# A hybrid decoder step on one Trainium2 core: split weights kept in DRAM, SSD products on two column tiles, another order for the last piece, and finer sample parts

## The chip, the cores and the metric

The kernel runs on one core of one Trainium2 chip. The metric is the device time of one launch in microseconds (us), as the median of several runs. The engines go by the names of the profile: PE (TensorE's matmuls) and PEld (its weight loads), DVE (VectorE), ACT (ScalarE), POOL (GpSimd) and SP (SyncE, whose queue issues every DMA of this kernel).

## The reference

One layer of a decoder with two parallel groups of heads, over a prompt of 2048 tokens and over 8 sample sequences of 4 tokens each, which start from given states. Everything is float32.

```python
D_MODEL, SEQ, DEC_BATCH, DEC_SEQ, CHUNK = 1024, 2048, 8, 4, 64
SSD_HEADS, SSD_HEAD_DIM, SSD_GROUPS, SSD_STATE = 16, 64, 2, 128
GDN_HEADS, GDN_HEAD_DIM, CONV_K = 8, 128, 4

def _layer(x, c, conv_s, h_ssm, conv_g, S_gdn, ...):
    shift, scale, gate = split(silu(c) @ w_ada + b_ada, 3)
    h = rmsnorm(x, norm_w) * (1 + scale) + shift
    z_s, xbc_raw, dt_raw, z_g, qkv_raw, a_raw, b_raw = split(h @ w_in, IN_SIZES)
    xbc, new_conv_s = causal_conv(xbc_raw, conv_s, ssd_conv_w, ssd_conv_b)      # conv of 4 taps, then silu
    y, new_h = ssd(xs, softplus(dt_raw + ssd_dt_bias), -exp(ssd_a_log), Bm, Cm, h_ssm)
    y = grouped_rmsnorm((y + xh * ssd_d) * silu(z_s), ssd_norm_w)
    qkv, new_conv_g = causal_conv(qkv_raw, conv_g, gdn_conv_w, None)
    q, k = l2norm(q) * 128 ** -0.5, l2norm(k)
    o, new_S = gated_delta(q, k, v, -exp(gdn_a_log) * softplus(a_raw + gdn_dt_bias), sigmoid(b_raw), S_gdn)
    o = rmsnorm(o, gdn_norm_w) * silu(z_g)
    return x + gate * (concat([y, o]) @ w_out), new_conv_s, new_h, new_conv_g, new_S

# ssd, per chunk:          y = ((C B^T) * L) (x dt) + exp(acum) C h;    h = h d + B^T (decay x dt)
# gated_delta, per chunk:  (I + M) [u, w] = rhs (a triangular solve);   v_new = u - w S
#                          o = q_dec S + (q k^T * decay) v_new;         S = S d + k_dec^T v_new
```

A final RMSNorm follows. The outputs are the tokens of prompt and samples and the new states of both.

## The kernel before, in words

**Arithmetic.** The two large projections run as three matmuls in the type float32r: each operand is split into a high part (a cast) and a low part (the rest after the cast is subtracted), and high x high, low x high and high x low are summed. The other products are plain float32 matmuls, each of which the profile shows as two passes (two matmul records, each with its weight load).

**In-projection.** The prompt is cut into 4 pieces of 512 tokens; the 32 sample tokens go with the last piece (so its conv tiles have 544 columns, done as twice 272). The columns of w_in are 52 blocks of 128. A block's weights are used in halves (4 of the 8 blocks along the model dimension, 256 KB), 104 halves a piece and 416 in all. `want(i0)` is called before half i0 is used and fetches up to `NH` = 4 halves ahead: a DMA into `xin` (3 buffers), a cast to `whi` on ACT (L488) and a subtraction to `wlo` on POOL (L489), 4 buffers each. Every piece loads and splits the same 104 halves again. A `conv_tile` uses two halves and ends in the causal conv on ACT and DVE (L525 to L538); in the last piece both halves are used for the first 272 columns, and then again for the rest. A `z_pair` uses four halves for two gate blocks (L608).

**The order of work.** TensorE works in exactly the order in which the code is emitted. `at(tau, f)` puts each step at a place of a common scale, 106 steps to a piece, and all steps are then emitted in the order of tau. For the other engines and for SP's queue a planner sets the order when the program is built, and `hold` only keeps a step behind what was emitted before it. The conv tiles and z pairs are the fills: 24 matmuls that need only weights, between which the steps of the chains below lie.

**Gated DeltaNet, `gdn_pair`**, four pairs of heads a piece, each a long chain: six conv tiles at so, transposes (L675) and k products (L737, L738), the triangular solve, in which U goes through DRAM into another layout (`ud`, `ul`), is solved by 31 small steps on DVE (`lane`, L779 to L786), goes back through DRAM (`dd`), and is put together by five small products (b2_0 to b2_4, L811 to L853), and then four chunks of three `hop`s each, which pass the state on: p1 (L866), p2 (L878) and p3 (L885), with DVE or ACT between them. The arguments `e` and `dch` of a pair set where the hops start and how many steps of tau lie between two.

**SSD, `ssd_group`**, two groups of eight heads a piece, four chunks of 128 tokens each: `load` and `decay` (POOL, ACT) make the decay matrices L, `first` transposes and scales, `second` multiplies (L1019, L1022), and `third` updates the state (L1032). L1022 is eight products, one a head: a 128 x 128 weight, 64 moving columns.

**The end.** After the fills of piece 3 come the last SSD chunks, the last hops and `ada_gate` (L195). Then the out-projection starts: `units`, each of which transposes a quarter of a token tile (`turn_q`) and runs 24 matmuls as two `mm_half`s (L1162); during the first 8 units w_out is loaded, scaled and split (`load_wo`, L1133, L1134, L237, L238). From the ninth unit on, after each unit, one step of `sample()` is taken: a generator that works through the 8 sample sequences (`gdn_sample` and `ssd_sample`), stopping at each `yield`. Its state updates multiply a masked operand `RS` (one buffer, made by four ACT instructions, L1284) into PSUM (L1416) and add it to the state.

## Time and profile before

| | |
|---|---|
| median of 3 runs | 2392.36 us (2386.32 to 2394.52) |
| the profiled execution | 2388.52 us, of which the span from the first to the last instruction is 2386.8 us |
| mean granted TensorE clock | 0.975 of full speed |
| busy: PE, DVE, POOL, ACT | 2235.7, 1596.7, 1150.7, 1090.4 us |
| DMA | 265.24 MB, 35.7% of 16 engines' span on the one queue |
| pieces 0, 1, 2, 3 (from the span's start) | 0 to 491.7, 928.6, 1363.6, 1848.6 us (the last fill) |
| tail to the first out-projection matmul | 1848.6 to 1919.3 us |
| out-projection and samples | 1919.3 to 2386.8 us |

How to read the rows: a group has its line, engine, operation, output and inputs by name, shapes and count, then busy time in us and the mean of one in ns, then the idle time of the engine before it and what ended it. A wait reads "engine line <- what it waited for: us in total, times, longest". A row of the timeline has its start and length in us. In a row of stages stand the stage and its length, then for each engine the busy time and the number of instructions, and at the end the granted clock, the DMA engines' share and GB/s.

### The profile page before, as it was taken

The numbers are of one execution on the slowest core, as the hardware profiler recorded it, in microseconds if no ns is written. First come the engines' busy times: TensorE is split into PE (matmuls) and PEld (weight loads), VectorE is DVE, ScalarE is ACT, GpSimd is POOL, SyncE is SP. The second block draws the span as 40 slices with busy tenths as digits, with TensorE's granted clock in tenths as the row PEclk, the third lists the DMA queues.
The fourth block names the chain that finished last, engine by engine and source line by source line (L and its number), as shares of the span: only waits on it lengthen the run. The fifth ranks groups of instructions, "written<-read, shape, count | busy, mean of one in ns | idle before, by whom it ended". The sixth has DMA issues, their size and how long they took to land.

```text
span 2386.8 us, 41614 instructions
## 1 busy us (share of the span) xinstructions
PE 2235.7 (94%) x14893; PEld 1901.8 (80%) x14893; DVE 1596.7 (67%) x3574; ACT 1090.4 (46%) x2938; POOL 1150.7 (48%) x1312
## 2 busy tenths in 40 slices
PE   7998999989999998999999899999999889999998
PEld 3687888878887887888788788999999468787776
DVE  2476768776867768786768877867786654434433
ACT  2534465455536455554645554636453341313211
POOL 3254665565548465655755555537453443232200
PEclk7999999999999999999999999999999999999999
DMA  6133333332334343333433432333233554434431
GB/s 216 58 96 90 101 115 114 111 103 87 102 96 128 105 121 95 94 109 101 118 103 92 126 93 75 93 86 107 80 92 86 182 188 151 145 112 142 153 130 51
DMA packets 236379, 265.24 MB, mean 111 GB/s; under 512 B 74216, under 2 KB 151784, under 8 KB 236172
## 3 DMA queue, kind: packets, MB, share of 16 engines
q1 hardware_dynamic: 236172, 262.59, 35.7%
q8 instruction: 117, 1.92, 0.3%
q14 instruction: 90, 0.74, 0.1%
HBM read 221.73 MB, written 40.78 MB: 110 GB/s over the span
## 4 chain that ended last, share of the span: by engine, by line
PE 57%; DVE 27%; ACT 4%; DMA 4%; issue 3%; POOL 3%; SPq 1%; POOLq 0%; DVEq 0%; ACTq 0%
PE pip L520 15%; PE pip L1162 13%; PE pip L608 10%; DVE tl L784 5%; DVE dl L786 5%; DVE cv L528 3%; PE pbk L1022 2%; DVE tr L528 2%; DVE dl L781 1%; PE pbk L168 1%; PE pbk L675 1%; PE pbk L1162 1%; DVE kT L528 1%; PE pch L1143 1%; PE pbk L737 1%
## 5 line engine op out<-in xcount | busy, mean ns | idle before, releaser
L489 POOL TENSOR_TENSOR wlo<-xin,whi 128x512 fp32r<-128x512 f32 x416 | 541.0, 1303 | 684.8 <-ACT whi L488 604.3
L520 PE MATMUL pip<-hhi,whi 128*128 128x512 f32 (+1 forms) x1440 | 536.6, 373 | 8.5 <-DVE kT L538 5.2
L520 PE MATMUL pip<-hhi,wlo 128*128 128x512 f32 (+1 forms) x1440 | 511.7, 355 | 0.0
L520 PE MATMUL pip<-hlo,whi 128*128 128x512 f32 (+1 forms) x1440 | 511.5, 355 | 0.0
L488 ACT CAST whi<-xin 128x512 fp32r<-128x512 f32 x416 | 254.9, 615 | 316.5 <-PE pip L520 131.4
L520 PEld LDWEIGHTS pip<-hhi,whi 128*128 128x128 f32 x1440 | 276.0, 192 | 49.8 <-issue 10.2
L520 PEld LDWEIGHTS pip<-hlo,whi 128*128 128x128 f32 x1440 | 276.0, 192 | 37.8 <-issue 5.3
L520 PEld LDWEIGHTS pip<-hhi,wlo 128*128 128x128 f32 x1440 | 274.8, 191 | 38.1
L608 PE MATMUL pip<-whi,hhi 128*128 128x256 f32 x1024 | 302.6, 295 | 1.8 <-DVE tr L538 1.7
L608 PE MATMUL pip<-whi,hlo 128*128 128x256 f32 x1024 | 291.3, 285 | 0.0
L608 PE MATMUL pip<-wlo,hhi 128*128 128x256 f32 x1024 | 290.2, 283 | 0.0
L608 PEld LDWEIGHTS pip<-whi,hhi 128*128 128x128 f32 x1024 | 197.2, 193 | 3.9 <-DVE tr L538 2.5
L1162 PE MATMUL pip<-wohi,mh 128*128 128x512 f32 x480 | 195.8, 408 | 1.8 <-ACT mh L1146 1.8
L608 PEld LDWEIGHTS pip<-whi,hlo 128*128 128x128 f32 x1024 | 196.8, 192 | 0.0
L608 PEld LDWEIGHTS pip<-wlo,hhi 128*128 128x128 f32 x1024 | 196.2, 192 | 0.1
L1162 PE MATMUL pip<-wohi,ml 128*128 128x512 f32 x480 | 188.9, 394 | 1.3 <-DVE ml L1153 1.3
L1162 PE MATMUL pip<-wolo,mh 128*128 128x512 f32 x480 | 187.6, 391 | 0.0
L528 DVE SCALAR_TENSOR_TENSOR tr<-pip,cw,tr 128x509 f32<-128x509 f32 (+6 forms) x240 | 152.6, 636 | 31.8 <-ACT tr L525 27.7
L784 DVE TENSOR_TENSOR tl<-dl,ul 128x60 f32<-128x60 f32 (+21 forms) x432 | 160.6, 372 | 8.7
L786 DVE TENSOR_TENSOR dl<-dl,tl 128x60 f32<-128x60 f32 (+21 forms) x432 | 150.9, 349 | 9.8
L528 DVE SCALAR_TENSOR_TENSOR cv<-pip,cw,cv 128x509 f32<-128x509 f32 (+2 forms) x180 | 114.6, 637 | 37.5 <-ACT cv L525 35.8
L1146 ACT CAST mh<-pch 128x512 fp32r<-128x512 f32 (+1 forms) x60 | 33.9, 564 | 167.6 <-PE pch L1143 167.6
(438 smaller groups left out, 4593.7 us busy)
## 6 DMA issues: line engine op xcount, KB each, us to landing
xin<-in_w_in SPq DMA_DIRECT2D x416, 256.0 KB
L<-rowsd SPq DMA_DIRECT2D x64, 256.0 KB
mx<-mixd SPq DMA_DIRECT2D x28, 512.0 KB
E<-rowsd SPq DMA_DIRECT2D x32, 256.0 KB
ul<-ud SPq DMA_DIRECT2D x64, 128.0 KB
mixd<-st SPq DMA_DIRECT2D x32, 256.0 KB
mixd<-z SPq DMA_DIRECT2D x16, 512.0 KB
x<-in_w_out SPq DMA_DIRECT2D x16, 512.0 KB
```

The lines of the kernel that those rows point to most:

```text
L168: pe.matmul(pa[0:9, :], sc[:, k, :], raw[:, k % 2, :], start=(k == 0), stop=(k == KD - 1))
L488: mark("ACT", s.copy(hi[:], rv))
L489: mark("POOL", g.tensor_tensor(lo[:], rv, hi[:], ALU.subtract))
L520: pe.matmul(pp, a[:, k, :], b[:, kk, cols], start=(i == 0), stop=(i == 23))
L528: v.scalar_tensor_tensor(u[:, c0 + dd:c0 + w], pp[:, 0:w - dd], cw[:, ci, k:k + 1], u[:, c0 + dd:c0 + w], ALU.mult, ALU.add)
L608: pe.matmul(out.rearrange("p (t c) -> p t c", t=2), a[:, k, cols], ws[b][:, :, k % 2, :], start=(first and k == 0 and e == 0), stop=(k == ...
L675: pe.transpose(pt[:, c * P:(c + 1) * P], src[:, c * P:(c + 1) * P], ident)
L784: v.tensor_tensor(tmp[:, 0:r, 0:w], _bc(dl[:, 0:r, m], [P, r, w]), ul[:, m, m + 1:32].unsqueeze(1).to_broadcast([P, r, w]), ALU.mult)
L786: v.tensor_tensor(dl[:, 0:r, m + 1:32], dl[:, 0:r, m + 1:32], tmp[:, 0:r, 0:w], ALU.add)
L1022: pe.matmul(py[:, i * 64:(i + 1) * 64], d["gms"][i // 4][:, i % 4, :], d["xdt"][:, i * 64:(i + 1) * 64], start=True, stop=True)
L1146: s.copy(mh[:, :, 0:n], ptv)
L1162: pe.matmul(pos[hb][0:m, :], a[:, k, 0:m], b[q * 4 + k][:, hb * 512:(hb + 1) * 512], start=(q == 0 and k == 0 and j == 0), stop=(q == 3 an ...
```

## The change

There are four parts, in one step.

1. **Weights kept split.** `whi` and `wlo` become one tile `w` of 512 KB (4 buffers). In piece 0 every second half, and in piece 1 the others, are stored in DRAM (`wsp`) when they are first used. A half that is stored is loaded from there straight into `w`, with no `xin`, cast or subtraction: 52 halves in piece 1 and all of pieces 2 and 3. Of the 416 splits 156 are left; there are 260 such loads and 104 stores.
2. **Two column tiles.** Each of the eight products of L1022 becomes two, for the output rows 0 to 63 and 64 to 127, with 64 columns of weights each.
3. **The table of the last piece.** In piece 3 the conv tiles of the SSD groups are spread, pairs 1 and 3 start 4 and 6 steps earlier, and the hops stand closer; the last pair of piece 2 gets closer hops too.
4. **Sample parts.** A step of `sample()` is taken after each `mm_half` instead of each unit, and the generators get more `yield`s: one state update a step, and two steps between a fetch and its use.

```diff
@@ want
-            n, hf, two = halves[j]
+            n, hf, two = key = halves[j]
+            w = mk(wp, [P, 2, 4, P], "w", F32R)
+            hi, lo = wt[j] = (w[:, 0, :, :], w[:, 1, :, :])
+            if key in wsp:
+                mark("SP", nc.sync.dma_start(w[:].bitcast(F32), wsp[key][:]))
+                continue
+            if j < len(halves) // NPC * 2 and (j % 2 == 0 or j >= len(halves) // NPC):
+                keep_w[j] = key, w
             raw = mk(xr, [P, T], "xin")
...
-            hi = mk(wp, [P, 4, P], "whi", F32R)
-            lo = mk(wp, [P, 4, P], "wlo", F32R)
-            mark("ACT", s.copy(hi[:], rv))
-            mark("POOL", g.tensor_tensor(lo[:], rv, hi[:], ALU.subtract))
-            wt[j] = (hi, lo)
+            mark("ACT", s.copy(hi, rv))
+            mark("POOL", g.tensor_tensor(lo, rv, hi, ALU.subtract))
+        if i0 in keep_w:
+
+            key, w = keep_w.pop(i0)
+            wsp[key] = wd = dram.tile([P, 2, 4, P], F32, name=nm("wsp"))
+            mark("SP", nc.sync.dma_start(wd[:], w[:].bitcast(F32)))
@@ ssd_group, second
                 for i in range(8):
-                    pe.matmul(py[:, i * 64:(i + 1) * 64], d["gms"][i // 4][:, i % 4, :],
-                              d["xdt"][:, i * 64:(i + 1) * 64], start=True, stop=True)
+                    hd = slice(i * 64, (i + 1) * 64)
+                    for t2 in (slice(0, 64), slice(64, 128)):
+                        pe.matmul(py[t2, hd], d["gms"][i // 4][:, i % 4, t2], d["xdt"][:, hd], start=True, stop=True)
@@ the table: arguments of gdn_pair are p, pair, so, zq, e, dch; of ssd_group p, group, tx(s), tf, tch, dch
-        lp = p == NPC - 1
+        late = p + 2 >= NPC
         gdn_pair(p, 0, base + 2, base + 14, 1.5, 1.32)
...
-        gdn_pair(p, 3, base + 78, base + 90, 0.5 if lp else 1.5, 1.3 if lp else 1.4)
+        if p + 1 < NPC:
...
+            gdn_pair(p, 3, base + 78, base + 90, 1 if late else 1.5, 1.2 if late else 1.4)
+        else:
+
+            ssd_group(p, 0, xs_at(18, 20, 38, 40), base + 42, base + 53, 4.6)
+            gdn_pair(p, 1, base + 22, base + 34, 0.3, 1.15)
+            gdn_pair(p, 2, base + 54, base + 66, 1.2, 1.3)
+            ssd_group(p, 1, xs_at(70, 88, 90, 92), base + 94, base + 105, 4.6)
+            gdn_pair(p, 3, base + 72, base + 84, 0.7, 1.2)
@@ gdn_sample: one yield more before the loop, one more after a fetch, and
                 nc.sync.dma_start(gdn_s[h0 + j, i], S[:])
-            yield
+                yield
@@ ssd_sample: one yield more after the loads, and
             for b in range(4):
-                if b % 2 == 0:
-                    yield
+                yield
@@ the out-projection's loop
             mm_half(u, 0)
+            if j >= 8:
+                next(extra, None)
             if j + 1 < len(units):
```

In the changed program the lines of before stand some lines further on (11 in the functions of gdn_pair, 11 to 12 in ssd_group). How the built program changes at the places that matter:

SP's queue in piece 3 at the third chunk of SSD group 0, before: loads of raw weights (xin) among the decay rows of the SSD and of a pair (L, E), the stores of the samples' conv columns (sraw) and a store of results (mixd).

```order
L485 DMA xin_18800<-in_w_in 128x512
L652 DMA E_18844<-rowsd_15774 128x512
L567 DMA sraw<-sr_18607 128x32
L652 DMA E_18884<-rowsd_15774 128x512
L485 DMA xin_18916<-in_w_in 128x512
L983 DMA L_18677<-rowsd_15774 128x4x128
L983 DMA L_18679<-rowsd_15774 128x4x128
L485 DMA xin_18922<-in_w_in 128x512
L567 DMA sraw<-sr_18745 128x32
L485 DMA xin_19106<-in_w_in 128x512
L950 DMA mixd<-st_18693 128x512
```

The same place in the changed program:

```order
L994 DMA L_18088<-rowsd_15348 128x4x128
L994 DMA L_18090<-rowsd_15348 128x4x128
L484 DMA w_18241<-wsp_2752 128x1024
L484 DMA w_18243<-wsp_7862 128x1024
L663 DMA E_18293<-rowsd_15348 128x512
L578 DMA sraw<-sr_18192 128x32
L663 DMA E_18333<-rowsd_15348 128x512
L961 DMA mixd<-st_18112 128x512
L484 DMA w_18371<-wsp_2922 128x1024
L484 DMA w_18373<-wsp_7974 128x1024
```

The weight loads now stand in pairs, the two halves of a conv tile, and go into w, whose buffer TensorE must have left, where a load into xin needed one that POOL had read.

POOL at the second chunk of SSD group 1 in piece 2, before: subtractions (L489) ahead of and between the decay (L989, L991) and the scalings (L1012, L1025, L936) of the SSD.

```order
L489 TENSOR_TENSOR wlo_14987<-xin_14984,whi_14986 128x512
L489 TENSOR_TENSOR wlo_15039<-xin_15036,whi_15038 128x512
L989 TENSOR_TENSOR L_14963<-L_14963,g_gc_10414 128x512
L989 TENSOR_TENSOR L_14965<-L_14965,g_gc_10414 128x512
L991 AFFINE_SELECT L_14963<-L_14963 128x512
L991 AFFINE_SELECT L_14965<-L_14965 128x512
L489 TENSOR_TENSOR wlo_15190<-xin_15187,whi_15189 128x512
L1012 TENSOR_TENSOR xD_15081<-xD_15081,rw 128x512
L1025 TENSOR_TENSOR xdt_15083<-xdt_15083,g_ed_10418 128x512
L936 TENSOR_TENSOR st_15250<-st_15250,xD_15081 128x512
```

The same place in the changed program:

```order
L1000 TENSOR_TENSOR L_14547<-L_14547,g_gc_10334 128x512
L1000 TENSOR_TENSOR L_14549<-L_14549,g_gc_10334 128x512
L1002 AFFINE_SELECT L_14547<-L_14547 128x512
L1002 AFFINE_SELECT L_14549<-L_14549 128x512
L1023 TENSOR_TENSOR xD_14657<-xD_14657,rw 128x512
L1037 TENSOR_TENSOR xdt_14659<-xdt_14659,g_ed_10338 128x512
```

The subtractions are gone, and the steps of the SSD follow on each other.

PE in the tail, after the last fill (a z pair, L608), before: hops of pair 2 (L885, L887, L866, L869, L878), an SSD chunk's products and ada_gate (L195) stand ahead of the first product of the last solve (L823), which comes twelve rows after these.

```order
L885 MATMUL pch_21733<-vp_21632,kd_18890 128x128 x2
L887 MATMUL po_21577<-vp_21632,A_19451 128x128 x2
L866 MATMUL pch_21752<-sg,kT_18553 128x128 x2
L869 MATMUL po_21755<-sg,qd_18986 128x128 x2
L195 MATMUL pip_21775<-xin_21776,sc 9x512
L195 MATMUL pip_21775<-xin_21779,sc 9x512
L878 MATMUL pch_21782<-xx_21758,U_19450 128x128 x2
L1019 MATMUL pbk_21792<-hs,cv_21437 128x512
L1022 MATMUL pbk_21794<-xdt_21726,L_21389 128x64 x4
L1022 MATMUL pbk_21794<-xdt_21726,L_21391 128x64 x4
```

The same place in the changed program: the last solve's first product (there L834) between the first two hops of a chunk.

```order
L877 MATMUL pch_20996<-sg,kT_17957 128x128 x2
L880 MATMUL po_20999<-sg,qd_18414 128x128 x2
L834 MATMUL pbk_21005<-dtx,U_19911 32x32 x16
L889 MATMUL pch_21034<-xx_21002,U_18856 128x128 x2
L845 MATMUL pbk_21040<-U_19911,p1x 32x32
```

The last solve's products moved ahead of ada_gate's and of an SSD chunk's.

More of the change, by code (lines that the diff above doesn't have):

```diff
@@ L471, in hymba_step_kernel @@
     wt = {}
+    wsp = {}
+    keep_w = {}
     def want(i0):
@@ L578, in quantum @@
             want(d["i0"] + j)
-            ws = [w[:].rearrange("p (t k) c -> p t k c", t=2) for w in wt[d["i0"] + j]]
+            ws = [w.rearrange("p (t k) c -> p t k c", t=2) for w in wt[d["i0"] + j]]
             for bk in range(2):
@@ L950, in ssd_fin, with ssd_group @@
         nc.sync.dma_start(mixd[rows_, gi * 512:(gi + 1) * 512], y)
-    def ssd_group(p, gi, tx, tf, tch, dch):
+    def ssd_group(p, gi, txs, tf, tch, dch):
         st = {}
@@ L960, in get_hc @@
             st["hc"] = halo_terms(24 + 6 * gi, 6)
-        at(tx - 1.5, get_hc)
+        at(txs[0] - 1.5, get_hc)
         def dst(i):
@@ L967, in ssd_group @@
         for i, n in enumerate((wn + 2, wn + 5, wn + 6, wn + 7, wn + 8, wn + 9)):
-            conv_tile(tx + 2 * i if i < 4 else tf + 6 * (i - 4), n, p, 24 + 6 * gi + i,
+            conv_tile(txs[i] if i < 4 else tf + 6 * (i - 4), n, p, 24 + 6 * gi + i,
                       lambda i=i: st["hc"][:, i, :], lambda i=i: dst(i))
@@ L1061, in hymba_step_kernel, with xs_at @@
                 at(base + 20.3 + 3 * i, lambda: next(gs, None))
-        lp = p == NPC - 1
+        def xs_at(*t):
+            return [base + i for i in t]
+        late = p + 2 >= NPC
         gdn_pair(p, 0, base + 2, base + 14, 1.5, 1.32)
-        ssd_group(p, 0, base + 18, base + 42, base + 53, 4.6)
-        gdn_pair(p, 1, base + 26, base + 38, 1.5, 1.4)
-        gdn_pair(p, 2, base + 54, base + 66, 1.5, 1.4)
-        ssd_group(p, 1, base + 70, base + 94, base + 105, 4.6)
-        gdn_pair(p, 3, base + 78, base + 90, 0.5 if lp else 1.5, 1.3 if lp else 1.4)
+        if p + 1 < NPC:
+            ssd_group(p, 0, xs_at(18, 20, 22, 24), base + 42, base + 53, 4.6)
+            gdn_pair(p, 1, base + 26, base + 38, 1.5, 1.4)
+            gdn_pair(p, 2, base + 54, base + 66, 1.5, 1.4)
+            ssd_group(p, 1, xs_at(70, 72, 74, 76), base + 94, base + 105, 4.6)
+            gdn_pair(p, 3, base + 78, base + 90, 1 if late else 1.5, 1.2 if late else 1.4)
[5 more added lines that the diff above has]
+            gdn_pair(p, 3, base + 72, base + 84, 0.7, 1.2)
         if p + 1 < NPC:
@@ L1419, in gdn_sample @@
                 nc.sync.dma_start(gdn_s[h0 + j, i], S[:])
-            yield
+                yield
     def ssd_prep(gi):
@@ L1470, in ssd_sample @@
             yield
+            yield
             for b in range(4):
@@ L1479, in ssd_sample @@
             for b in range(4):
-                if b % 2 == 0:
-                    yield
+                yield
                 pu = psum("bk")
```

## The prediction

> **What bounds the kernel now.** I read the page first (engines, chain), then busy time by stage, then who TensorE waits for, and last the timelines of the touched lines.
>
> ```profile
> PE 2235.7 (94%) x14893; PEld 1901.8 (80%) x14893; DVE 1596.7 (67%) x3574; ACT 1090.4 (46%) x2938; POOL 1150.7 (48%) x1312
> PE 57%; DVE 27%; ACT 4%; DMA 4%; issue 3%; POOL 3%; SPq 1%; POOLq 0%; DVEq 0%; ACTq 0%
> core 0: 2386.8 us, clock 0.975
> ```
>
> TensorE is the bound: 94% busy, and the time not busy is only 151 us. The chain still runs through DVE for 27%, so where TensorE does wait, it is mostly for DVE. The granted clock of 0.975 says that another 2.5% of the span (60 us) went by at less than the full clock.
>
> Busy time by stage (pieces 0 to 3, the tail of piece 3, the start of the out-projection, the rest of it):
>
> ```profile
> core 0: us, PE busy (x) PEld busy (x) DVE busy (x) ACT busy (x) POOL busy (x), PEclk, DMA share, GB/s
> 491.70:928.60 436.90, 418.75 (x2865) 361.67 (x2863) 329.55 (x727) 234.22 (x625) 255.21 (x279) 0.98 0.36 106
> 928.60:1363.60 435.00, 418.90 (x2882) 362.54 (x2882) 331.79 (x727) 231.85 (x623) 253.19 (x277) 0.98 0.36 106
> 1363.60:1848.60 485.00, 459.24 (x3926) 441.11 (x3927) 368.03 (x997) 246.44 (x755) 248.10 (x263) 0.98 0.30 88
> 1848.60:1919.30 70.70, 54.86 (x364) 32.25 (x363) 44.27 (x82) 29.32 (x81) 27.55 (x31) 0.93 0.53 169
> 1963.00:2386.80 423.80, 403.25 (x1986) 315.81 (x1984) 174.68 (x307) 99.75 (x247) 94.16 (x137) 1.00 0.38 127
> ```
>
> Span less PE busy gives the idle time: 18.2 us in piece 1, 16.1 in piece 2, 25.8 in piece 3, 15.8 in the tail. Each of pieces 1 to 3 also loses up to 2% to the clock (9, 9 and 10 us). So there are two ways to gain: less work on TensorE, or fewer waits.
>
> **The change, part by part.** All sums stand against the profiled execution (span 2386.8 us, its own time 2388.5 us), which is 3.9 us under the median of 2392.4 us; the forecast is moved up by those 3.9 us.
>
> *SSD products on two column tiles.* This is work on TensorE itself.
>
> ```profile
> 324.22 1.89 PE L1022 MATMUL pbk<-xdt,L 128*128 128x64 f32 x16
> 325.92 0.37 PE L608 MATMUL pip<-whi,hhi 128*128 128x256 f32 x1
> 213.12 0.28 PE L608 MATMUL pip<-whi,hlo 128*128 128x256 f32 x1
> 213.32 1.15 PE L845 MATMUL pbk<-dt,U 128*64 128x64 f32 x16
> 214.40 0.65 PE L675 MATMUL pbk<-cs,tr 128*128 128x128 f32 x4
> 2003.35 0.27 PE L1366 MATMUL pbk<-L,kq 128*64 128x128 f32 x1
> 2003.36 0.27 PE L1366 MATMUL pbk<-L,wC 128*64 128x128 f32 x1
> 2003.46 0.27 PE L1366 MATMUL pbk<-L,kq 128*64 128x128 f32 x1
> 2003.46 0.27 PE L1366 MATMUL pbk<-L,wC 128*64 128x128 f32 x1
> ```
>
> From its first start to the next line's first, the old product takes 1.70 us for 16 passes of 128 columns of weights. L845 has the new shape (64 columns of weights, 64 moving) in one column group: 16 passes in 1.08 us, with the change of shape at both ends. L1366 alternates two column groups as the new code does, and its passes start in pairs 0.11 us apart. So 32 new passes are 16 pairs. If a pair costs what one pass of L845 costs, a product takes 1.08 us and saves 0.62; 32 products (4 pieces, 2 groups, 4 chunks) save 20 us. If nothing overlapped, 32 passes would take 2.16 us: 15 us more than now. I take 20 saved, since L1366 is the same pattern on the same matrix.
>
> L845's row already holds what the change of shape costs. The Trainium skill, TensorEngine Tiling (Array Packing), Key Properties, says that changing the tiling mode drains TensorE. Taken to the letter, no matmul would overlap its neighbour at either switch. In the rows they do, by 0.08 us on the way in (213.12 + 0.28 against 213.32) and 0.07 on the way out (1.15 against 1.08); by the rule a product would then take 1.23 us and the term be 15 us, by the rows it is 20.
>
> *Weights kept split in DRAM.* 416 casts on ACT and 416 subtractions on POOL become 156 each. In exchange there are 104 stores of 512 KB, in pieces 0 and 1, and 260 loads of 512 KB take the place of loads of 256 KB. Neither engine bounds anything by its own load. What matters is DVE:
>
> ```profile
> 689.98 0.23 DVE L784 TENSOR_TENSOR tl<-dl,ul 128x65 f32<-128x65 f32 x1
> 689.99 1.37 POOL L489 TENSOR_TENSOR wlo<-xin,whi 128x512 fp32r<-128x512 f32 x1 [2.39 <-ACT whi L488]
> 690.25 1.19 DVE L786 TENSOR_TENSOR dl<-dl,tl 128x65 f32<-128x65 f32 x1
> L489 POOL TENSOR_TENSOR wlo<-xin,whi 128x512 fp32r<-128x512 f32 x416 | 541.0, 1303 | 684.8 <-ACT whi L488 604.3 <-ACT halo L536 47.7 <-ACT sr L566 11.2
> L784 DVE TENSOR_TENSOR tl<-dl,ul 128x60 f32<-128x60 f32 (+21 forms) x432 | 160.6, 372 | 8.7
> L786 DVE TENSOR_TENSOR dl<-dl,tl 128x60 f32<-128x60 f32 (+21 forms) x432 | 150.9, 349 | 9.8
> PE pch L878 <- DVE xx L873: 5.6, 2, 3.8
> PE pch L866 <- DVE sg L890: 4.3, 3, 2.4
> ```
>
> A small DVE step of the lane solve takes 0.23 us alone and 1.19 us when a POOL subtraction began before it: it ends when POOL does. Over 864 such steps the means (372 and 349 ns) lie above 230 ns by 112 us. L489 is 541 of POOL's 1151 us, and 260 of 416 go: between 33 us (its share of POOL) and 70 us (all of it) of DVE time come back, nearly all in pieces 1 to 3. The last two rows, TensorE's longest waits in piece 2, are waits for DVE steps that stand among those lane steps. With the subtractions all gone from pieces 2 and 3 and half gone from piece 1, I take half of the idle and clock time of piece 2 (25 us, so 12), a third of piece 3's (36 us, so 12) and a sixth of piece 1's (27 us, so 4): 28 us.
>
> Against it stand the loads, which now write the buffer from which TensorE reads and so wait until it has left that buffer:
>
> ```profile
> 1235.96 2.93 DMA xin<-in_w_in
> 1848.63 3.63 DMA x<-in_w_out
> 1856.78 5.00 DMA x<-in_w_out
> 1824.57 0.37 PE L520 MATMUL pip<-hhi,whi 128*128 128x272 f32 x1
> 1830.68 0.61 PE L885 MATMUL pch<-vp,kd 128*128 128x128 f32 x4
> SPq L485 <- POOL wlo L489: 276.5, 96, 9.3
> SPq L791 <- DVE dl L786: 17.3, 3, 8.5
> SPq L983 <- PE pbk L1022: 25.9, 12, 7.7
> SPq L567 <- ACT sr L566: 24.4, 16, 4.9
> ```
>
> 256 KB landed in 2.9 us; 512 KB took 3.6 to 5.0. In piece 2 a load has three halves of cover, 3 x 435/104 = 12.5 us, and is hidden. In piece 3 a conv tile uses two halves over 48 matmuls, 6.1 us by the two L520 and L885 rows; the next-but-one tile's two loads start when it ends and have one tile of cover. That is 6.1 us against 5.0 and the issue of two loads: just enough, unless the queue stands at another wait (the SP rows of pieces 2 and 3, up to 8.5 us). For 36 conv tiles I charge 10 us between ends of 0 (all covered) and 104 (every tile 2.9 us late, worked out below). So this part is -18 us. Behind a waiting load stand, on SP, the loads of L and E, the lane solve's moves through DRAM and the stores to mixd, and each is late by as much; but the same queue already waits there for POOL, 276.5 us in pieces 2 and 3. The stores cost nothing: one is issued as its half's first matmul comes up and has until the buffer's reuse, again three halves; without that cover the cast of the next half would wait up to 5.0 us. In piece 2 the wider loads add 104 x 0.26 MB, 63 GB/s on top of 106, by proportion a DMA share of 0.57; the tail ran at 0.53.
>
> The Trainium skill, DMA: Bandwidth & Descriptors, puts a DMA at about 2.0 us and its bytes over 436 GB/s. As an estimate 512 KB would then land in 3.2 us and nothing be late (the part would be -28); the rows show up to 5.0 us, and I go by them.
>
> *Last piece in another order.* The last pair's six conv tiles and its z move ahead of three SSD tiles, so its lane solve and its hops come six steps of the table earlier against the last fill.
>
> ```profile
> PE pbk L823 <- DVE L L1014: 7.4, 1, 7.4
> PE pch L885 <- ACT vp L881: 2.2, 3, 1.2
> ```
>
> These head TensorE's waits in the tail. The tail holds 15.8 us of idle time and 7% of clock loss (5 us), 21 us in all, which is the most this can give; a chain of four chunks of hops still ends it. I take 10, with 0 and 21 as ends. Inside piece 3 the work only changes places, nothing is added. The hops stand closer (1.15 to 1.3 steps for 1.3 to 1.4, and 1.2 for 1.4 at the end of piece 2), so a hop's matmuls have less other work between them; the DVE time freed above covers it, and without that cover I would add two waits of 1.4 to 3.8 us, like those of piece 2.
>
> *Sample parts per half.*
>
> ```profile
> PE pbk L1416 <- ACT RS L1284: 10.9, 8, 1.4
> 2057.62 0.40 PE L1416 MATMUL pbk<-RS,wA 128*128 128x512 f32 x1
> 2059.38 0.50 PE L1416 MATMUL pbk<-RS,wA 128*128 128x512 f32 x1 [1.37 <-ACT RS L1284]
> ```
>
> Two state updates stood back to back, and the second waited for its RS, a single buffer: 8 waits, 10.9 us. Now half a unit (12 matmuls, about 2.8 us) lies between them, against 1.4 us of wait. I take 10 of the 10.9. The extra steps after a fetch keep its lead at one unit. All sample work now ends some units sooner, at the same cost.
>
> Sum: -20 -18 -10 -10 = -58 us. 2388.5 becomes 2330.5; on the median's footing 2334 us.
>
> **The rivals.**
>
> *The time comes back as waits for DVE* (chance 0.15). A shorter product leaves less cover over the same DVE work: 76% busy in pieces 1 to 3, and the hops wait for DVE already. Against it: DVE gets 33 to 70 us back. If all 20 us return, the sum is -38: 2354 us.
>
> *The column tiles do not overlap* (0.08): the product does not become cheaper, though it is on two tiles. L845's own rows are serial; L1366 speaks against it. 15 us more in place of 20 less: -23, so 2369 us.
>
> *Late weights* (0.08), the slower side. In piece 3 the two loads of a tile land after the tile before it is done. With a pair at 9 us in place of 5 (a load queued behind the SP waits above), each of 36 tiles is 2.9 us late: 104 us against the gains of 28 + 20 + 10 + 10 = 68, so 2428 us. It decides from 68/36 = 1.9 us a tile. Against it: the DMA share there is only 0.30, and half of the tiles have other matmuls between them.
>
> *All the waits go* (0.07): if pieces 2 and 3 lose all 61 us of idle and clock loss and the tail its 21, the sum is -20 -61 -4 -21 -11 = -117: 2275 us.
>
> **How the numbers follow.** The forecast keeps 0.62, with 2305 to 2365 as its own spread (late loads 0 to 25, waits half or double). The range of 2300 to 2378 takes in the first two rivals and leaves out most of the other two. A change below 0.3% (7 us) cannot be told from none here. Of the forecast and the three rivals on its side 0.88 end faster by more than that and 0.04 within it; of late weights 0.01 end within it and 0.07 slower: 0.88, 0.05, 0.07.
>
> **What would show it.** The product's line should start 32 passes in pairs within 1.1 us; POOL's subtraction should be x156 and L784's mean in pieces 2 and 3 near 230 ns; the wait on L1416 should be gone; the tail from the last z matmul to the first out-projection matmul should be near 60 us. I am wrong if TensorE's waits in pieces 2 and 3 name a DMA into w, or if its waits for DVE grow.

## The result, and the profile after

The changed kernel takes 2329.39 us (median of 4 runs, 2327.78 to 2332.32) against 2390.77 us (2386.32 to 2394.52) for the kernel before on the same chip: ratio 0.9746, 95% interval 0.9729 to 0.9762, so 57 to 65 us less. The forecast was 2334 us. The total came out, though not by its terms: as the runs below show, one of the four was too small, two came to nothing, and that these misses cancel is luck.

The page of the changed kernel, engines and clock:

```profile
PE 2200.8 (95%) x15405; PEld 1864.9 (80%) x15405; DVE 1481.9 (64%) x3574; ACT 953.1 (41%) x2680; POOL 826.7 (36%) x1052
core 0: 2326.1 us, clock 0.979
```

TensorE's busy time fell by 35 us and its idle time (span less busy) from 151 to 125 us. DVE lost 115 us and POOL 324 us of busy time. By stage, each cut at the same matmul in both programs (the 817th and 1633rd and the last z matmul of L608, now L619; the first and the 133rd out-projection matmul of L1162, now L1185), first of before, then of after:

```profile
0.00:564.80 564.80, 514.17 (x3195) 418.10 (x3195) 373.16 (x796) 276.09 (x707) 294.83 (x337) 0.95 0.36 110
564.80:1081.10 516.30, 495.97 (x3357) 427.14 (x3357) 395.16 (x875) 276.42 (x739) 300.06 (x326) 0.99 0.35 105
1081.10:1848.30 767.20, 730.31 (x5844) 680.41 (x5840) 581.47 (x1468) 392.64 (x1140) 409.18 (x442) 0.98 0.33 96
1848.30:1919.30 71.00, 55.16 (x367) 32.54 (x365) 44.42 (x83) 29.57 (x82) 27.55 (x31) 0.93 0.53 168
1919.30:1962.90 43.60, 36.78 (x157) 27.69 (x157) 27.71 (x48) 15.89 (x25) 24.80 (x43) 0.96 0.63 203
1962.90:2386.80 423.90, 403.35 (x1986) 315.91 (x1984) 174.78 (x307) 99.75 (x247) 94.26 (x137) 1.00 0.38 127
```

```profile
0.00:551.50 551.50, 507.10 (x3307) 409.44 (x3307) 363.12 (x799) 271.91 (x699) 288.39 (x334) 0.95 0.53 174
551.50:1049.10 497.60, 485.83 (x3503) 415.13 (x3501) 362.68 (x875) 232.33 (x658) 193.23 (x240) 1.00 0.63 199
1049.10:1791.30 742.20, 715.74 (x6045) 665.45 (x6040) 506.95 (x1469) 306.89 (x976) 193.35 (x270) 0.99 0.52 159
1791.30:1859.50 68.20, 49.74 (x424) 28.02 (x422) 44.17 (x82) 30.82 (x86) 36.97 (x48) 0.94 0.55 179
1859.50:1897.10 37.60, 36.65 (x157) 28.52 (x157) 26.82 (x48) 14.14 (x19) 20.22 (x28) 0.92 0.73 223
1897.10:2326.06 428.96, 405.79 (x1986) 318.30 (x1984) 178.18 (x306) 97.01 (x245) 94.52 (x133) 0.99 0.39 126
```

The first three stages (pieces 0 to 3 together) lost 13, 19 and 25 us, 57 of the 61. The tail lost 2.8 us and the first units of the out-projection 6.0; the rest of it, where the sample parts stand, grew by 5.1. The costliest groups of the changed kernel on POOL and DVE, POOL's subtractions and the two lane steps (L784 and L786 before):

```profile
L496 POOL TENSOR_TENSOR w<-xin,w 128x512 fp32r<-128x512 f32 x156 | 202.6, 1301 | 378.3 <-ACT w L495 344.8 <-DVE vs L735 9.3 <-ACT halo L547 8.9
L795 DVE TENSOR_TENSOR tl<-dl,ul 128x60 f32<-128x60 f32 (+21 forms) x432 | 121.0, 280 | 9.3
L797 DVE TENSOR_TENSOR dl<-dl,tl 128x60 f32<-128x60 f32 (+21 forms) x432 | 119.1, 276 | 9.0
```

The first lane step alone in the third stage (DVE's busy time, count, clock), before and after:

```profile
1081.10:1848.30 767.20, 64.70 (x189) 0.98 0.33 96
1049.10:1791.30 742.20, 43.38 (x189) 0.99 0.52 159
```

A product (now L1035) in the timeline of the changed kernel:

```profile
316.39 1.02 PE L1030 MATMUL pbk<-hs,cv 128*128 128x512 f32 x2
317.35 1.15 PE L1035 MATMUL pbk<-xdt,L 128*64 128x64 f32 x32
318.43 0.50 PE L619 MATMUL pip<-w,hhi 128*128 128x256 f32 x2
```

In the third stage (piece 3 and most of piece 2) L795's mean is 43.38 us / 189 = 230 ns, against 342 for the same 189 steps before. From its first start to the next line's a product takes 1.08 us (before: 1.70 to 1.73, the median of the 32). The line ahead of it starts 0.96 us before; in the kernel before that was 0.86, from the row that follows to the L1022 shown above at 324.22:

```profile
323.36 1.02 PE L1019 MATMUL pbk<-hs,cv 128*128 128x512 f32 x2
```

### The profile page after: what moved, and what is told of

Read it like the earlier page. It is cut to its first block, busy times and chain, and to the rows that moved or that the text cites. A ratio compares the mean times of both kernels' runs of the same rounds, so it can differ in the third digit from the quotient of the medians.

```text
span 2326.1 us, 41856 instructions
## 1 busy us (share of the span) xinstructions
PE 2200.8 (95%) x15405; PEld 1864.9 (80%) x15405; DVE 1481.9 (64%) x3574; ACT 953.1 (41%) x2680; POOL 826.7 (36%) x1052
## 5 line engine op out<-in xcount | busy, mean ns | idle before, releaser
L531 PE MATMUL pip<-hhi,w 128*128 128x512 f32 (+1 forms) x2880 | 823.7, 362 | 6.7 <-DVE kT L549 4.9
L531 PEld LDWEIGHTS pip<-hhi,w 128*128 128x128 f32 x2880 | 515.0, 190 | 85.0 <-issue 6.9
L531 PE MATMUL pip<-hlo,w 128*128 128x512 f32 (+1 forms) x1440 | 509.8, 354 | 0.0
L619 PE MATMUL pip<-w,hhi 128*128 128x256 f32 x2048 | 382.6, 287 | 0.3 <-DVE cv L549 0.3
L496 POOL TENSOR_TENSOR w<-xin,w 128x512 fp32r<-128x512 f32 x156 | 202.6, 1301 | 378.3 <-ACT w L495 344.8
L619 PEld LDWEIGHTS pip<-w,hhi 128*128 128x128 f32 x2048 | 316.5, 190 | 2.4 <-DVE cv L549 0.5
L531 PEld LDWEIGHTS pip<-hlo,w 128*128 128x128 f32 x1440 | 274.5, 191 | 36.9 <-issue 4.5
L619 PE MATMUL pip<-w,hlo 128*128 128x256 f32 x1024 | 289.4, 283 | 0.0
L1185 PE MATMUL pip<-wohi,mh 128*128 128x512 f32 x480 | 195.3, 407 | 7.4 <-ACT mh L1169 7.2
L619 PEld LDWEIGHTS pip<-w,hlo 128*128 128x128 f32 x1024 | 194.8, 190 | 0.0
L1185 PE MATMUL pip<-wohi,ml 128*128 128x512 f32 x480 | 189.7, 395 | 1.1 <-DVE ml L1176 1.0
L1185 PE MATMUL pip<-wolo,mh 128*128 128x512 f32 x480 | 189.1, 394 | 0.8 <-DVE wolo L238 0.8
L539 DVE SCALAR_TENSOR_TENSOR tr<-pip,cw,tr 128x509 f32<-128x509 f32 (+5 forms) x240 | 152.8, 637 | 40.2 <-ACT tr L536 37.1
L795 DVE TENSOR_TENSOR tl<-dl,ul 128x60 f32<-128x60 f32 (+21 forms) x432 | 121.0, 280 | 9.3
L797 DVE TENSOR_TENSOR dl<-dl,tl 128x60 f32<-128x60 f32 (+21 forms) x432 | 119.1, 276 | 9.0
L1185 PEld LDWEIGHTS pip<-wohi,mh 128*128 128x128 f32 x480 | 91.4, 190 | 27.0 <-ACT mh L1169 7.8
L1185 PEld LDWEIGHTS pip<-wohi,ml 128*128 128x128 f32 x480 | 91.0, 190 | 22.8 <-DVE ml L1176 3.0
L1185 PEld LDWEIGHTS pip<-wolo,mh 128*128 128x128 f32 x480 | 91.4, 190 | 18.2 <-DVE wolo L238 1.1
L1169 ACT CAST mh<-pch 128x512 fp32r<-128x512 f32 (+1 forms) x60 | 33.7, 562 | 166.4 <-PE pch L1166 166.3
```

The source lines that it names most:

```text
L496: mark("POOL", g.tensor_tensor(lo, rv, hi, ALU.subtract))
L531: pe.matmul(pp, a[:, k, :], b[:, kk, cols], start=(i == 0), stop=(i == 23))
L539: v.scalar_tensor_tensor(u[:, c0 + dd:c0 + w], pp[:, 0:w - dd], cw[:, ci, k:k + 1], u[:, c0 + dd:c0 + w], ALU.mult, ALU.add)
L619: pe.matmul(out.rearrange("p (t c) -> p t c", t=2), a[:, k, cols], ws[b][:, :, k % 2, :], start=(first and k == 0 and e == 0), stop=(k == ...
L795: v.tensor_tensor(tmp[:, 0:r, 0:w], _bc(dl[:, 0:r, m], [P, r, w]), ul[:, m, m + 1:32].unsqueeze(1).to_broadcast([P, r, w]), ALU.mult)
L797: v.tensor_tensor(dl[:, 0:r, m + 1:32], dl[:, 0:r, m + 1:32], tmp[:, 0:r, 0:w], ALU.add)
```

## The experiments

All ratios are to the kernel before, measured beside it on the same chip; the time in the fourth column is the ratio's distance from 1 times 2391 us.

| kernel | median us | ratio (95% interval) | against before, us |
|---|---|---|---|
| the change | 2329.4 | 0.9746 (0.9729 to 0.9762) | -61 |
| column tiles alone | 2406.5 | 1.0064 (1.0048 to 1.0080) | +15 |
| weights kept split alone | 2350.4 | 0.9827 (0.9807 to 0.9848) | -41 |
| last piece's order alone | 2393.5 | 1.0005 (0.9994 to 1.0016) | +1 |
| sample parts per half alone | 2394.4 | 1.0009 (0.9998 to 1.0021) | +2 |
| weights kept split + column tiles | 2330.8 | 0.9756 (0.9740 to 0.9771) | -58 |
| the change without the halves | 2329.2 | 0.9745 (0.9730 to 0.9760) | -61 |
| the change + wide idle POOL steps | 2391.9 | 1.0013 (1.0001 to 1.0025) | +3 |
| the change + small idle POOL steps | 2351.7 | 0.9821 (0.9807 to 0.9836) | -43 |
| without the halves + last scaling on POOL | 2331.3 | 0.9760 (0.9744 to 0.9776) | -57 |
| before + shorter product, no second tile | 2380.9 | 0.9948 (0.9934 to 0.9961) | -12 |
| the change, passes in turn | 2345.1 | 0.9800 (0.9784 to 0.9815) | -48 |
| the change, all halves kept in piece 0 | 2333.1 | 0.9745 (0.9732 to 0.9759) | -61 |

### Each part alone

The four kernels apply one part of the diff each to the kernel before. Column tiles (the hunk in the SSD chunk's second step):

> The kernel before with one edit: each SSD product as 32 passes on two column tiles. Theory from the two traces: a product is 0.62 us shorter from its first start to the next line's, and enters 0.09 us later, so 0.53 to 0.55 us net, x32 = -17 us (2374). Rival 'back as waits for DVE', since the subtractions on POOL are still there: TensorE's two hop lines wait longer by about as much, -5 to 0 us (2386 to 2391). The prediction's own term was -20.

Weights kept split (the hunks in want and quantum):

> The kernel before with one edit: the weights kept split in DRAM. Theory: pieces 0 to 3 lost 57 us in the changed kernel and the column tiles explain 18 of them, so this edit alone gives -35 to -40 us (2351 to 2356), with no wait of TensorE that names a load into w. The prediction's term was -28 for fewer DVE waits and +10 for late loads, -18 (2373). Rival 'it needs the tiles': below -15 us alone.

The last piece's order (ssd_group's list of steps, and the table of gdn_pair and ssd_group calls):

> The kernel before with one edit: the last piece's table (and piece 2's last pair with it). Theory: the tail and the start of the out-projection together lost 8.8 us, so -9 us (2382), if the hops that now stand closer find DVE free. Rival: with the POOL subtractions still in the pieces the closer hops wait for DVE and the edit alone gives 0 or up to +8 us. The prediction's term was -10.

The sample parts (the yields and the second call of next(extra)):

> The kernel before with one edit: sample parts after each half of a unit. Theory: the eight waits on RS (10.9 us) go, but TensorE waits instead for the loads of h_ssm, for DVE's wA and gr, and each gap of over 3 us brings a stretch at half clock: +2 to +6 us (2393 to 2397), with the out-projection after its start 3 to 5 us longer. The prediction's term was -10 (2381).

Added up, the four give -23 us, not -61. The column tiles alone made the kernel slower, which neither theory had allowed for. The page with the tiles alone, then with the split weights alone:

```profile
PE 2226.3 (93%) x15405; PEld 1881.1 (78%) x15405; DVE 1608.7 (67%) x3574; ACT 1090.7 (45%) x2938; POOL 1154.0 (48%) x1312
core 0: 2405.5 us, clock 0.971
```

```profile
PE 2224.7 (95%) x14893; PEld 1896.0 (81%) x14893; DVE 1483.2 (63%) x3574; ACT 956.3 (41%) x2680; POOL 815.9 (35%) x1052
core 0: 2343.2 us, clock 0.978
```

With the tiles alone each product does start its 32 passes within 1.08 us, yet TensorE idles 179 us against 151 before (2405.5 - 2226.3), and its busy time falls by 9 us only, as the granted clock drops from 0.975 to 0.971. The longer waits are spread over many lines, and the rows still name DVE and ACT; no one of them explains the 28 us. One that the prediction showed for piece 2, over the whole run now (before: 16.9, 11, 3.9):

```profile
PE pch L866 <- DVE sg L890: 21.4, 11, 3.9
```

With the split weights alone DVE falls by 113 us, about as much as in the changed kernel (115), and TensorE's idle time by 33 us, to 118; the time is about what their theory had. The order and the halves are within the measurement of nothing. In its one profile the order alone takes 6.8 us off the tail and the start of the out-projection (69.5 + 38.3 against 71.0 + 43.6) and gives 5.9 back in the third stage ahead of them (773.1 against 767.2).

Did loads of kept weights come late, as the prediction charged? No row of TensorE's waits names one. With the split weights alone one row names no releaser at all ("issue"):

```profile
PE pip L531 <- issue: 6.5, 2, 3.5
```

The longer of its two waits, as the timelines of DVE and PE have it:

```profile
1361.90 0.41 DVE L549 SCALAR_TENSOR_TENSOR kT<-pip,kT 128x240 f32<-128x240 f32 x1 [0.72 <-ACT pip L548]
1362.41 0.56 PE L531 MATMUL pip<-hhi,w 128*128 128x272 f32 x1 [3.50 <-issue]
```

TensorE starts again 0.10 us after DVE's L549 has ended (1362.31), the last step on the accumulator pip of a conv tile, and L549 had waited for ACT's L548. By the trace's semaphores TensorE waited there for DVE and for the load of w issued at 1348.89, which had landed by 1352.1. The other wait ends in the same way, L549 at 1485.68 and TensorE at 1485.78. On SP's queue there is a gap ahead of the first one, from 1351.2 to 1359.64, in which it stands at a store to mixd, but the loads of w behind it, issued from 1360.05 on, are not those that TensorE needed; at the second wait the next load of w is issued at 1485.80, when TensorE has started again. So what stands here is a wait for an accumulator, by way of ACT and DVE, and no late weight is shown. One such wait of 1.8 us is left in the changed kernel (L549 ends at 1682.56, TensorE starts at 1682.66).

### Together, and against the out-projection's waits

> The kernel before with two edits: weights kept split, and the products on two column tiles. Alone they gave -41 us and +15 us. Theory 'the tiles pay only once DVE and POOL have room': with the subtractions gone the tiles bring their 0.55 us x 32 = 18 us, so 2350 - 18 = 2332 us (2327 to 2338), and TensorE's waits for the px transposes and the hops do not grow. Rival 'the tiles cost on their own account' (the switch of shape, the clock): 2350 + 15 = 2365 us.

With DVE relieved, the tiles give what their work says (18 us): 2350.4 to 2330.8, 19.5 us by the medians and 17 by the ratios. These two parts alone are the result; the other two add nothing to them that can be told.

> The changed kernel with the sample parts as before (once a unit). Theory: the halves gave +3 us alone and the out-projection behind its start is 5 us longer in the changed kernel, so this is 3 to 5 us faster than the changed kernel: 2324 to 2327 us, with the eight waits on RS (10.9 us) back and the waits for h_ssm (6.7 us) and wA (3.5 us) gone. Rival, the prediction's term: 10 us slower than the changed kernel, 2339.

Neither: the halves are worth nothing in either direction (ratio 0.9745 without, 0.9746 with). Of the 5.1 us by which the rest of the out-projection grew, 3.2 stay without them (427.1 us, against 429.0 with them and 423.9 before). In the trace of the changed kernel's out-projection the eight waits are indeed gone, and others stand in their place:

```profile
PE pip L1185 <- ACT mh L1169: 7.2, 1, 7.2
PE po L1499 <- DMA L<-in_h_ssm: 6.7, 3, 3.6
PE pbk L1508 <- DVE wA L1293: 3.5, 1, 3.5
PE pbk L1407 <- DVE gr L1396: 2.0, 2, 1.3
PE pbk L1441 <- ACT RS L1307: 1.0, 2, 0.6
```

The RS waits fell from 10.9 to 1.0 us, but the waits for h_ssm, wA and gr rose from 1.6 to 12.2. A load of h_ssm writes a buffer that the store of an earlier state must have left: SP's wait for that store grew from 4.8 us (9 times, 1.1 at most) to 23.7 (10 times, 4.9 at most). Each of the two gaps of over 3 us was followed by a stretch of 3.4 us at half clock (here the one behind the wait for h_ssm, PEclk 0.50), which eight waits of 1.4 us had not brought (clock 1.00 in that stage before):

```profile
2111.00:2114.30 3.30, 3.30 (x9) 1.62 (x8) 0.73 (x2) 0.66 (x2) 1.06 (x1) 0.50 0.00 0
```

The first row of those waits is the other half of "where did the expected gain go". TensorE is done with the tail at 1852.3 us and waits 7.2 us for the first mh cast, which on ACT stands behind the eight scaling steps of the last pair's norm, and these wait for POOL's ob:

```profile
1856.51 2.44 ACT L917 ACTIVATE qd<-qd,ob 128x128 f32<-128x128 f32 x8 [2.33 <-POOL ob L937]
1858.86 0.56 ACT L1169 CAST mh<-pip 128x512 fp32r<-128x512 f32 x1
```

In the kernel before this wait was 1.8 us, and so it is with the split weights and the tiles alone. With the new order alone it is 7.2 as well. So one kernel took those eight steps off ACT:

```
-                    s.mul(qd[:, i, :], qd[:, i, :], co[:, i:i + 1])
+                    if p == NPC - 1 and pr == 3:
+                        g.tensor_scalar(qd[:, i, :], qd[:, i, :], co[:, i:i + 1], None, ALU.mult)
+                    else:
+                        s.mul(qd[:, i, :], qd[:, i, :], co[:, i:i + 1])
```

> The changed kernel with the sample parts as before, and with the scaling of the last pair's eight heads-by-chunks (the eight ACT steps of 2.4 us in all that stand ahead of the first mh cast on ACT and wait for POOL's ob) done on POOL. Theory: the first mh cast then waits only for ACT's st step at 1854.1 us and comes 4.6 us earlier, so TensorE's wait of 7.2 us at the start of the out-projection becomes 2.6, and the kernel is 4 to 5 us faster than the one without the halves: 2320 to 2323. Rival: the weights' loads and splits behind it end as late as before and take the gain back in the first units: within 1 us of the one without the halves.

Waits from the tail on, of that kernel:

```profile
PE pip L1188 <- ACT mh L1172: 2.4, 1, 2.4
PE pbk L1188 <- DVE ml L1179: 3.1, 2, 1.8
PE pip L1188 <- DVE ml L1179: 1.8, 2, 1.5
```

The wait fell from 7.2 to 2.4 us as expected, and the time did not get shorter (0.9760 against 0.9745): the rival. The first units then wait for ml, the next step of the same chain, 4.9 us against 2.0 in the kernel without the halves, and the out-projection from its 133rd matmul on is 4 us longer in the one profile.

### Is it POOL's wide steps that hold up DVE?

Both kernels add idle work on POOL to the changed kernel, beside each of the 260 loads of a kept weight; nobody reads what it writes:

```
             if key in wsp:
                 mark("SP", nc.sync.dma_start(w[:].bitcast(F32), wsp[key][:]))
+                idle = mk(xr, [P, T], "xin")[:].rearrange("p (a b) -> p a b", a=2)
+                two_cs = cs[:, 0:256].unsqueeze(1).to_broadcast([P, 2, 256])
+                mark("POOL", g.tensor_tensor(idle, two_cs, two_cs, ALU.subtract))
                 continue
```

> The changed kernel with 260 idle subtractions on POOL: beside each load of a kept weight POOL subtracts a constant tile from itself (128x512) into a buffer that nobody reads. No weight waits for them, ACT and the loads stay as in the changed kernel. Theory 'POOL's subtractions held up DVE': DVE's busy time comes back by most of the 115 us that it lost, TensorE's waits for DVE with it, and the time rises by 25 to 45 us (2354 to 2374). Rival 'the gain came from the casts on ACT or from the loads that no longer wait for POOL': DVE's sum may rise, the time rises by under 8 us (to 2337 at most).

The small ones (the same place, five of 128x8 in place of the one of 128x512):

```
+                idle = mk(xr, [P, T], "xin")
+                for i in range(5):
+                    c8 = slice(8 * i, 8 * i + 8)
+                    mark("POOL", g.tensor_tensor(idle[:, c8], cs[:, c8], cs[:, c8], ALU.subtract))
```

> The changed kernel with POOL kept as busy as by the 260 idle subtractions of 128x512 (278 us), but by small ones: five of 128x8 (about 0.2 us each) beside each load of a kept weight, 1300 in all. DVE's steps behind a 128x8 step of POOL lose next to nothing in the traces (1.5 us over 100 us of POOL time, against 179 over 542 for the subtractions of 128x512). Theory 'a wide POOL step holds up DVE': DVE's busy time rises by under 15 us and the time by under 10 us (2339 at most). Rival 'POOL's own results come late because its queue is fuller': the time rises as with the wide ones, to 2365 or more.

The wide ones took back 64 us by the ratios, all that the change had gained and more than expected; the small ones 18, between what the two theories had. The page, the group of idle steps and the first lane step in the third stage, cut as above, with the wide ones:

```profile
PE 2220.7 (93%) x15405; PEld 1879.8 (79%) x15405; DVE 1551.6 (65%) x3574; ACT 951.1 (40%) x2678; POOL 1095.4 (46%) x1312
```

```profile
L487 POOL TENSOR_TENSOR xin<-cs 128x512 f32<-128x512 f32 x260 | 277.7, 1077 | 14.5 <-PE pbk L325 5.4 <-ACT xsq L262 2.8
```

```profile
1095.90:1857.50 761.60, 55.94 (x189) 0.98 0.51 155
```

And with the small ones:

```profile
PE 2212.5 (94%) x15405; PEld 1872.5 (80%) x15405; DVE 1496.9 (64%) x3574; ACT 951.1 (40%) x2678; POOL 1047.6 (45%) x2352
```

```profile
L488 POOL TENSOR_TENSOR xin<-cs 128x8 f32<-128x8 f32 x1300 | 233.5, 213 | 12.1 <-PE pbk L325 1.8 <-ACT halo L551 0.9 <-ACT xsq L262 0.3
```

```profile
1068.40:1811.70 743.30, 43.57 (x189) 0.99 0.53 159
```

With POOL busy for about as long (1095 and 1048 us), DVE grew by 70 us behind the wide steps and by 15 behind the small ones. In the third stage the wide ones add 19.4 us (761.6 against 742.2) and 12.6 us to the lane step alone (55.9 against 43.4); the small ones add 1.1 and 0.2 us. The number of casts and loads is the same in all three kernels. So most of the part's gain comes from DVE no longer held up by wide POOL steps, and the rival (a fuller POOL queue) has the smaller share, 18 of 64 us. By the stages of the one profile each, the wide steps add 13.1, 33.7 and 19.4 us to the first three and the small ones 10.8, 8.5 and 1.1, so what only the wide ones bring lies in the second and third. Ahead of the third stage the idle steps also take turns with the raw loads in the xin buffers; how much of the small ones' time is the queue and how much these buffers stays open.

The Trainium skill, SBUF — State Buffer, Who interferes with whom, says that a DVE instruction with two SBUF inputs contends with a GpSimd instruction that reads SBUF, and that one blocks for the other's whole instruction. The lane steps read two SBUF tiles, and behind wide steps the traces agree. Behind narrow ones they don't: POOL's L99 raises 128x8 elements to a power in 1.64 us, longer than a subtraction of 128x512 (1.30 us), and lane steps of DVE run inside it at their usual length, as here in the changed kernel:

```profile
1454.38 1.64 POOL L99 TENSOR_TENSOR ob<-oa,mhalf 128x8 f32<-128x8 f32 x1
1454.73 0.23 DVE L797 TENSOR_TENSOR dl<-dl,tl 128x64 f32<-128x64 f32 x1
1455.33 0.23 DVE L795 TENSOR_TENSOR tl<-dl,ul 128x75 f32<-128x75 f32 x1
```

So what DVE loses goes with how much a POOL step reads and writes, and neither with how long the step takes nor with POOL's sum. The two idle kernels alone could not tell width from length, as their steps differ in both (128x512 in 1077 ns, 128x8 in 213).

### What the tiles' gain is, and what else it needs

```
                 for i in range(8):
                     hd = slice(i * 64, (i + 1) * 64)
-                    for t2 in (slice(0, 64), slice(64, 128)):
-                        pe.matmul(py[t2, hd], d["gms"][i // 4][:, i % 4, t2], d["xdt"][:, hd], start=True, stop=True)
+                    pe.matmul(py[0:64, hd], d["gms"][i // 4][:, i % 4, 0:64], d["xdt"][:, hd], start=True, stop=True)
+                for i in range(8):
+                    hd = slice(i * 64, (i + 1) * 64)
+                    pe.matmul(py[64:128, hd], d["gms"][i // 4][:, i % 4, 64:128], d["xdt"][:, hd], start=True, stop=True)
```

> The changed kernel with the 32 passes of each product in another order: the 16 of output rows 0 to 63 first, then the 16 of rows 64 to 127, so that neighbours stand on the same column tile. Theory 'the gain is that two column tiles run at a time': the product takes 2.16 us from its first start to the next line's, 1.08 more, and the time rises by 20 to 40 us (2349 to 2369). Rival 'a pass of 64 columns of weights is simply cheaper': 1.08 us as now, and 2329 within 4 us.

In its timeline the next line starts 1.82 us after the product's first pass (the median of the 32 is 1.83); its page follows:

```profile
317.49 0.97 PE L1034 MATMUL pbk<-xdt,L 128*64 128x64 f32 x13
...
318.46 0.92 PE L1037 MATMUL pbk<-xdt,L 128*64 128x64 f32 x13
319.31 0.50 PE L619 MATMUL pip<-w,hhi 128*128 128x256 f32 x2
```

```profile
PE 2223.9 (95%) x15405; PEld 1888.2 (81%) x15405; DVE 1486.2 (63%) x3574; ACT 953.1 (41%) x2680; POOL 820.0 (35%) x1052
```

The order of the passes decides, so the gain is that two column tiles run at a time. In turn, a pass takes 1.83/32 = 0.057 us, and a product 0.75 us more and not 1.08. That is 24 us of TensorE's work (busy +23), of which 13 show in the ratio (0.9800 against 0.9746): idle time fell by 8.

> The kernel before with a shorter product that has no second column tile: four matmuls of 128 columns in place of eight of 64 (8 passes of about 0.11 us in place of 16), which leaves out the decay of every second head (each pair of heads uses the first one's). TensorE loses 0.8 us of work a product, 27 us in all, and no change of shape is added. Theory 'before the weights were kept split, TensorE's time is given back as waits for DVE, POOL and as clock, whatever shape the product has': 2385 to 2405 us, like the column tiles alone (2406). Rival 'the column tiles themselves cost something': 2364 to 2371 us.

```
-                for i in range(8):
-                    pe.matmul(py[:, i * 64:(i + 1) * 64], d["gms"][i // 4][:, i % 4, :],
-                              d["xdt"][:, i * 64:(i + 1) * 64], start=True, stop=True)
+                for i in range(0, 8, 2):
+                    pe.matmul(py[:, i * 64:(i + 2) * 64], d["gms"][i // 4][:, i % 4, :],
+                              d["xdt"][:, i * 64:(i + 2) * 64], start=True, stop=True)
```

A product in its timeline, its page and its clock:

```profile
546.18 1.05 PE L1022 MATMUL pbk<-xdt,L 128*128 128x128 f32 x8
547.07 0.60 PE L675 MATMUL pbk<-cs,kT 128*128 128x128 f32 x4
```

```profile
PE 2214.4 (93%) x14637; PEld 1879.8 (79%) x14637; DVE 1608.7 (68%) x3574; ACT 1090.7 (46%) x2938; POOL 1153.4 (48%) x1312
core 0: 2380.7 us, clock 0.971
```

Between the two theories: 27 us less work (0.89 for 1.73 us a product), 12 us less time, with idle time up by 15 us (2380.7 - 2214.4 = 166.3, against 151.1) and the clock down to 0.971 as with the tiles. So in the kernel before about half of what TensorE saves comes back even with no second tile (11 to 18 of 27 us by the interval of the time). Why the tiles alone end 26 us above this kernel (2406.5 against 2380.9), though they save only 9 us less work, is not settled: DVE is equally busy in both (1608.7), and beside the split weights the tiles bring 17 to 20 us.

The last one keeps all of piece 0 (the changed kernel: half of piece 0, the rest in piece 1):

```
-            if j < len(halves) // NPC * 2 and (j % 2 == 0 or j >= len(halves) // NPC):
+            if j < len(halves) // NPC:
```

> The changed kernel with all 104 halves stored in piece 0, so that piece 1 loads all of its weights split, and 104 subtractions on POOL (and casts on ACT) remain in place of 156. Theory: the 260 subtractions that went were worth 41 to 62 us, 0.16 to 0.24 us each, so 52 more give 8 to 12 us: 2317 to 2321. Rival: piece 0 already moves 174 GB/s, the 52 stores that move into it make its raw loads late, and the time stays within 4 us of 2329 or rises.

POOL lost another 72 us of busy time (to 754.2) and DVE 8 us (to 1474.2), and the time did not change: the rival's number. By stages the first is 3.7 us longer and the second 1.6 shorter; that late raw loads are the reason is not shown. No kernel here is faster than the changed one by more than can be told.

## Why the prediction was right, and where it was not

The total of -58 us (measured: -57 to -65) rests on two terms that were too large and one that was too small. That they cancelled is luck; the mechanism of the two parts that gave the result was right.

- *Column tiles, -20:* right in the changed kernel (17 to 20 us beside the split weights), with 1.08 us a product and pairs that overlap as L1366's did. It was not a property of the part: alone it is +15, worse than the first rival, the time comes back as waits for DVE, had it. The ground on which the prediction set that rival aside, "DVE gets 33 to 70 us back", held, and the term needed it. That saved time comes back in the kernel before, whatever shape saved it, is shown (11 to 18 of 27 us); the rest of the tiles' loss alone stays open.
- *The switch of shape:* the rows of L845 hid some of it. The entry costs 0.10 us (0.96 against 0.86), so a product came to 1.18 us. The Trainium skill, TensorEngine Tiling (Array Packing), Key Properties, taken to the letter had given 1.23, the rows 1.08; the measurement stands nearer to the rule. With 1.73 - 1.08 - 0.10 = 0.55 us saved the term would have been 18.
- *No overlap, +15:* its price was too high. Serial passes take 0.057 us, not the 0.0675 of L845's row, so a product of 1.83 + 0.10 us against 1.73 would have cost 6 us of work and not 15.
- *Weights kept split, -28 + 10:* mis-sized, alone it is -41. The mechanism was right (L784's mean fell to 230 ns in the third stage, the subtractions are x156), but DVE's busy time fell by 113 us and not by 33 to 70. The two lane lines alone gave 71 of the 115 in the changed kernel (160.6 + 150.9 to 121.0 + 119.1), the top end of that bound; the other DVE steps, which were not counted, gave the rest. Counted over all DVE steps, as for the small idle steps above, 179 us were lost behind the subtractions before, and 260/416 of that is 112. The +10 was charged for late loads, and none is shown.
- *Last piece, -10:* failed. The tail and the start of the out-projection lost 8.8 us together, but the tail is 68 and not 60, and the split weights with the tiles have nearly all of it without the new order (67.0 + 39.9, against 68.2 + 37.6 with it). The order alone is +1 (-1 to +4), and with it the kernel is not measurably faster than with the first two parts alone (0.9745 against 0.9756). The wait of 7.4 us on L1014's L fell to 3.3 (on L1025's, for L1044) and one of 7.2 on the mh cast came in place of 1.8; the step "a chain of four chunks of hops still ends it" missed the norm behind the hops, on which ACT's next cast waits.
- *Sample parts, -10:* failed. The waits on RS went, as forecast. What failed is "The extra steps after a fetch keep its lead": the loads of h_ssm, held up by the stores that must leave their buffers, and DVE's wA and gr became the late ones.
- *The clock:* the reading that 2.5% of the span, 60 us, went by at less than the full clock is off. The stretches at clock 0.50 add up to 122 us before, and 60 us is about what they cost.

## What to carry to other kernels

Two changes to one schedule need not be worth the sum of what each brings alone: the column tiles cost 15 us by themselves and brought 17 to 20 once DVE, for which TensorE waits, had been relieved, and a shorter product of another shape kept only 12 of its 27 us without that. Ask of each term which engine must have room for it, and test the parts alone and together before crediting them. Where two elementwise engines share work, look for wide steps on the second one, and count what they cost over all steps of the first; narrow steps cost little here, even long ones. A wait that a profile calls "issue" is not yet a late DMA: see what ended just before it did.

## What was not expected of the hardware

- Two gaps of TensorE of 3.5 us were each followed by a stretch of about 3.4 us at a granted clock of 0.50, while eight gaps of 1.4 us were not. In the traces of before and after, every gap of over 3 us had such a stretch, and of those between 1.4 and 3 us some had (1.65 us up to 739.2 before) and some not (2.80 us up to 967.3). Trading short waits for fewer long ones gave back part of what it saved.
- Passes of 64 columns of weights take 0.057 us on one column tile and 0.034 us each when two tiles alternate, so a pair costs 1.2 times one pass and not once.
- 260 idle POOL steps, 278 us of POOL time whose results nobody reads, made the kernel 64 us slower; 1300 short ones of 233 us in all made it 18 slower. A POOL step of 128x8 that takes 1.64 us did not hold up the lane steps of DVE that ran inside it.
